# Attention, retention and mixture-of-experts block on one Trainium2 core: the weight slots are cut differently, the record tile gets four buffers, and sixteen identity matmuls stand at the start

## Chip, cores and metric

The kernel is one program on one core of one Trainium2 chip. Its time is device microseconds (us) of one execution. Engines: PE (TensorE; PEld is its weight load), DVE (VectorE), ACT (ScalarE), POOL (GpSimd) and SP (SyncE, which issues nearly all DMAs here, in order, from one queue).

## What is computed

One encoder layer on 512 tokens of width 1024, in float32:

```
xn = rms_norm(x)
proj = xn @ w_in            # attention q/k/v in 3 groups, retention q/k/v/gate, branch gates
A = dilated window attention, 3 groups (window, dilation), 8 heads of 64;
    the groups' outputs are summed with softmax weights of their log-sum-exp
B = retention in chunks of 128, forward + backward, 8 heads, group norm, swish gate
h = x + (sigmoid(gA) * (A @ W_A) + sigmoid(gB) * (B @ W_B)) @ w_out
hn = rms_norm(h)
h = h + MoE(hn)             # 64 experts, top group of 8, top 2 in it; w1, w3: 1024x512, w2: 512x1024
out = rms_norm(h)
```

Every expert's w1, w3 and w2 are read whole: 16 groups of four experts, 12 blocks of 2 MB each.

## The kernel before, in words

**Start.** SP loads the four token tiles `h[:, tt, :]` (128 tokens each, L111) and between them the first two `raw` tiles (512 KB of w_in each, L105). For each token tile ACT squares and sums it (`xs_start`, L223), POOL takes a power (L154), DVE finishes the reciprocal root (L137 to L144) and scales the tile (L232), PE transposes it against `ident` (L196), ACT casts the transposed half (`xH`, L199) and DVE takes the remainder (`xL`, L200). This order is written by hand for DVE, ACT and POOL (`manual_schedule`, L219); everything outside such a block is placed by a list scheduler, which may put other work between. So it is with the retention decays: `dec` is loaded by two small DMAs (L338, L339), and a chain of some 25 small DVE operations (L341 to L357) makes `lg` of it, from which ACT makes the table `xi` (L375). L420 multiplies the router weights `wr` by `nwm`.

**Projections.** `project` multiplies the tokens by 512 columns of a weight matrix. A unit is one `raw` tile (256 rows): ACT makes `wH` (L212), DVE the remainder `wL` (L213), each for two halves of 128 rows (called k0 and k1 here), and PE then runs 24 matmuls: for four accumulators two halves times `x,wH`, `x,wH`, `x,wL` (L267 to L269, or L273 to L275). `raw` has two buffers, `wH` and `wL` three, the accumulators `acc` four. `evac_gate` (L676, ACT) empties the accumulators of a branch gate. The unit spoken of below is the first of branch gate 2, `raw_4115`, `wH_4117`, `wL_4118` in the program before.

**Records.** Attention groups 1 and 2 leave a record (`rec`, 264 KB) per token tile, which goes to DRAM (L660). Between branch gates 1 and 2 the records are combined: per token tile two `rec` are loaded (L697), DVE multiplies three records by their weights (L701), POOL adds the second and the third to the first (L704, two adds), DVE takes a reciprocal (L706) and multiplies (L707). `rec` has two buffers before.

**Experts.** `wtile` hands out slots of 2 MB: first `wA` five times, then `big` and `wk` (each once), then `x0`, `x1` (the tiles that held the transposed tokens) and `wB` twice; after that the ring of nine goes round without `big` and `wk`. A group takes eight blocks of w1 and w3 (j = 0 to 7, L979), then four of w2 (L1049). `wA`, `big` and `wk` lie on the right side of SBUF, in room that the attention's pools leave (`right.close()`, L762); `wk` lay beyond the others, at the edge to the free strip. `x0` and `x1` come free as w_out's matmuls end, `wB` when `mixer.close()` (L918) has given back the left side. Slots are filled in the order in which they are handed out.

Of the kernel before, what the change touches and what calls it, by code (L numbers as in the profile page):

```python
# [10 lines left out]
F32 = mybir.dt.float32  # L11
# [10 lines left out]
P = 128  # L22
# [13 lines left out]
CAP = 32  # L36
EG = 4
NGRP = NE // EG
NWA = 5
NWB = 2  # L40
SLOT = 4096


# [27 lines left out]
def hybrid_block(ctx, tc, a, out):  # L71
# [27 lines left out]
    nc.scalar.dma_start(out=nwx, in_=a["norm_mix_w"].rearrange("o (k p) -> p (o k)", p=P))  # L99
    xp = ctx.enter_context(tc.tile_pool(name="xp", bufs=1, side="left"))  # L100
    lw = mixer.enter_context(tc.tile_pool(name="lw", bufs=1, side="left"))

    def load_raw(w, r0, c0):
        raw = lw.tile([P, 2, 512], F32, name="raw", bufs=2)
        nc.sync.dma_start(out=raw, in_=w[r0:r0 + 2 * P, c0:c0 + 512].rearrange("(k p) n -> p k n", p=P))  # L105
        return raw

# [7 lines left out]
    nc.vector.memset(one1, 1.0)  # L115
    nc.scalar.activation(one1, one1, AF.Square)
    make_identity(nc, ident)
    nc.gpsimd.iota(ranks, pattern=[[1, CAP]], base=1, channel_multiplier=0, allow_small_or_imprecise_dtypes=True)
    nc.gpsimd.iota(iota, pattern=[[1, NE]], base=0, channel_multiplier=0, allow_small_or_imprecise_dtypes=True)
    tri = left.tile([P, P], BF16, name="tri")  # L120
# [501 lines left out]
    for g in range(3):  # L622
        qT, kT = qk_tiles()
        project_in(512 * g, None, rotary_to(qT, g > 0))
        project_in(1536 + 512 * g, None, rotary_to(kT, g > 0, kP))
        vt = rp.tile([P, 2080], F32, name="v", bufs=3)
        v4 = vt.rearrange("p (t h d) -> p t h d", t=NT, h=NH)
        nc.gpsimd.memset(v4[:, :, :, HD:HD + 1], 1.0)

        def evac_va(tt, ps, v4=v4):  # L630
            nc.scalar.copy(v4[:, tt, :, 0:HD], ps.rearrange("p (h d) -> p h d", h=NH))
        project_in(3072 + 512 * g, orders[g], evac_va)

        if g == 0:
            windows(qT, v4)
            continue
        for t in range(NT):
            rec_t = at.tile([P, REC], F32, name="rec", bufs=2)
            rec = rec_t[:, :]
            for h0 in range(0, NH, 4):  # L640
                ps = tmp()
                sm = rp.tile([P, 512], F32, name="sd", bufs=6)
                ts = slice(t * P, (t + 1) * P)
                for i in range(0, 4, 2):
                    nc.tensor.matmul(ps[:, i * P:(i + 2) * P], qT[:, (h0 + i) // 2, ts], kP[:, (h0 + i) // 2, :, ts],  # L645
                                     start=True, stop=True)
                for i in range(4):
                    cs = slice(i * P, (i + 1) * P)
                    probs(rec, h0 + i, ps[:, cs], sm[:, cs],
                          masks[:, 3 * HD:3 * HD + P] if g == 1 else masks[:, 9 * HD:])  # L650
                prT = transposed_probs(ps, sm, 4)
                po_ps = tmp()
                for i in range(4):
                    oc = i * (HD + 1)
                    for f in range(2):
                        qs = slice(i * P + f * HD, i * P + (f + 1) * HD)
                        nc.tensor.matmul(po_ps[f * HD:(f + 1) * HD, oc:oc + HD + 1], prT[:, qs], v4[:, t, h0 + i, :],
                                         start=True, stop=True)
                nc.scalar.copy(rec[:, h0 * (HD + 1):(h0 + 4) * (HD + 1)], po_ps[:, :4 * (HD + 1)])
            nc.sync.dma_start(out=scr[g - 1].rearrange("(l r) c -> r l c", r=4)[t], in_=rec)  # L660
# [32 lines left out]
    for tt in range(NT):  # L693
        r3 = [rec0[:, tt, :]]
        for g in (1, 2):
            rb = at.tile([P, REC], F32, name="rec", bufs=2)
            nc.sync.dma_start(out=rb, in_=scr[g - 1][tt * P:(tt + 1) * P, :])  # L697
            r3.append(rb[:, :])
        r3 = [r_[:, :NH * (HD + 1)].rearrange("p (h d) -> p h d", h=NH) for r_ in r3]
        for g in range(3):  # L700
            nc.vector.tensor_tensor(r3[g], r3[g], al[:, g, tt, :].unsqueeze(2).to_broadcast([P, NH, HD + 1]),  # L701
                                    op=ALU.mult)
        for g in (1, 2):
            nc.gpsimd.tensor_tensor(r3[0], r3[0], r3[g], op=ALU.add)  # L704
        ds = at.tile([P, NH], F32, name="dsum")
        nc.vector.reciprocal(ds, r3[0][:, :, HD])  # L706
        nc.vector.tensor_tensor(yatt[:, tt, :].rearrange("p (h d) -> p h d", h=NH), r3[0][:, :, 0:HD],  # L707
                                ds.unsqueeze(2).to_broadcast([P, NH, HD]), op=ALU.mult)
# [60 lines left out]
    mh = pre.tile([P, NT, NE], BF16, name="mh")  # L769
    big = ctx.enter_context(tc.tile_pool(name="big", bufs=1, side="right"))  # L770
    wA = ctx.enter_context(tc.tile_pool(name="wA", bufs=NWA, side="right"))
    early = ExitStack()
    wk = early.enter_context(tc.tile_pool(name="wk", bufs=1, side="right"))

    def gather(t, oh_t, gp, js=range(NK)):

# [116 lines left out]
    for c in range(2):  # L893
        def evac_o(tt, ps, c=c):
# [10 lines left out]
            else:  # L905
# [4 lines left out]
                    router_rank(tt - 1)  # L910
        project(a["w_out"], 0, NK, 512 * c, mH, mL, nat, evac_o, groups=None if c == 0 else ((0,), (2,), (4, 6)),
                early=True)
    gather_first(1)
    gather_first(2, range(4))
    router_rank(NT - 1)
# [278 lines left out]
```

## Time and profile before

| | |
|---|---|
| runs | 1619.35, 1622.75, 1623.1 us; median 1622.75 |
| profiled execution | 1621.28 us, of which 1619.6 us are the span of the trace |
| PE busy | 1338.7 us (83%) |
| data moved | 476.14 MB, 294 GB/s over the span; 427 to 429 GB/s in nearly every slice from 729 us on |
| chain that ended last | PE 55%, DMA 38%, DVE 4% |

The span falls into two parts. Up to about 680 us PE is busy nearly all the time and the DMA engines are half idle; from about 690 us on the DMA engines are busy all the time and PE partly waits. In the profile's tables a busy share is in tenths of a slice of 40.5 us.

### The profile page before, as it was taken

The numbers are of one execution on the slowest core, as the hardware profiler recorded it, in microseconds if no ns is written. First come the engines' busy times: TensorE is split into PE (matmuls) and PEld (weight loads), VectorE is DVE, ScalarE is ACT, GpSimd is POOL, SyncE is SP. The second block draws the span as 40 slices with busy tenths as digits, with TensorE's granted clock in tenths as the row PEclk, the third lists the DMA queues.
The fourth block names the chain that finished last, engine by engine and source line by source line (L and its number), as shares of the span: only waits on it lengthen the run. The fifth ranks groups of instructions, "written<-read, shape, count | busy, mean of one in ns | idle before, by whom it ended". The sixth has DMA issues, their size and how long they took to land.

```text
span 1619.6 us, 20935 instructions
## 1 busy us (share of the span) xinstructions
PE 1338.7 (83%) x8707; PEld 825.7 (51%) x8707; DVE 562.0 (35%) x1241; ACT 317.8 (20%) x614; POOL 208.4 (13%) x151
## 2 busy tenths in 40 slices
PE   7999999999999999997775785776776676677674
PEld 6878887697977788743331331331332232233133
DVE  7556564464857335441220220221121021022014
ACT  5332333335354423210000000000000000000002
POOL 2213452260716011000000000000000000000001
PEclk9999999999999999999897987998897888898897
DMA  6334243233434423899999999999999999999995
GB/s 183 104 88 108 92 140 96 53 117 93 118 112 133 149 79 132 349 405 428 428 427 429 428 428 428 428 427 429 428 428 428 429 427 429 428 427 428 428 427 224
DMA packets 70980, 476.14 MB, mean 294 GB/s; under 512 B 14240, under 2 KB 14752, under 8 KB 46112
## 3 DMA queue, kind: packets, MB, share of 16 engines
q1 hardware_dynamic: 69840, 474.74, 73.3%
q8 instruction: 70, 1.15, 0.3%
q14 instruction: 30, 0.25, 0.0%
q10 hardware_dynamic: 1040, 0.00, 0.0%
HBM read 459.96 MB, written 4.26 MB: 287 GB/s over the span
## 4 chain that ended last, share of the span: by engine, by line
PE 55%; DMA 38%; DVE 4%; ACT 1%; issue 1%; POOL 1%; SPq 0%; DVEq 0%; ACTq 0%; POOLq 0%
DMA wa<-in_moe_w2r_dram 23%; DMA x<-in_moe_w2r_dram 10%; PE acc L267 6%; PE acc L268 6%; PE acc L269 6%; PE tmp L778 6%; PE acc L979 5%; PE acc L274 4%; PE acc L273 4%; PE acc L275 4%; DMA wa<-in_moe_w_dram 2%; DMA wB<-in_moe_w2c_dram 2%; PE tmp L1031 2%; PE acc L1049 2%; PE tmp L1032 2%; PE tmp L645 1%
## 5 line engine op out<-in xcount | busy, mean ns | idle before, releaser
L979 PE MATMUL acc<-wa,xT 128*32 128x512 f32 x1120 | 156.6, 693 | 69.5 <-DMA wa<-in_moe_w_dram 69.5
L213 DVE SCALAR_TENSOR_TENSOR wL<-raw,nwx,wH 128x512 fp32r<-128x512 f32 x152 | 149.1, 1014 | 118.8 <-ACT wH L212 117.4
L267 PE MATMUL acc<-x,wH 128*128 128x512 f32 x416 | 170.1, 409 | 3.1 <-ACT kT L676 3.1
L269 PE MATMUL acc<-x,wL 128*128 128x512 f32 x416 | 167.8, 403 | 0.0
L268 PE MATMUL acc<-x,wH 128*128 128x512 f32 x416 | 167.8, 403 | 0.0
L212 ACT ACTIVATE wH<-raw,nwx 128x512 fp32r<-128x512 f32 x152 | 103.2, 717 | 174.8 <-PE acc L268 81.3
L1049 PE MATMUL acc<-wa,hid 128*32 128x512 f32 x560 | 88.8, 764 | 54.4 <-DMA wa<-in_moe_w2r_dram 50.2
L274 PE MATMUL acc<-wL,x 128*128 128x512 f32 x320 | 127.8, 399 | 0.1
L273 PE MATMUL acc<-wH,x 128*128 128x512 f32 x320 | 127.4, 399 | 0.1
L275 PE MATMUL acc<-wH,x 128*128 128x512 f32 x320 | 127.4, 398 | 0.0
L154 POOL TENSOR_TENSOR rr<-rv,mhalf 128x1 f32<-128x1 f32 x8 | 5.0, 644 | 925.0 <-ACT jk L1088 914.0
L979 PEld LDWEIGHTS acc<-wa,xT 128*32 128x32 f32 x1120 | 34.2, 119 | 171.4 <-DMA wa<-in_moe_w_dram 93.7
L1011 DVE SCALAR_TENSOR_TENSOR hid<-hid,gsl,acc 128x512 f32<-128x512 f32 x16 | 12.0, 748 | 308.0 <-issue 149.5
L778 PE MATMUL tmp<-oh,h 128*128 128x128 f32 x960 | 111.2, 277 | 0.3 <-DVE big L1033 0.3
L778 PEld LDWEIGHTS tmp<-oh,h 128*128 128x128 f32 x960 | 108.3, 192 | 4.7 <-DVE big L1033 4.7
L1024 DVE TENSOR_TENSOR yp<-acc,yp 128x512 fp32r<-128x512 f32 (+2 forms) x35 | 22.5, 643 | 239.3 <-ACT yp L1023 239.2
L267 PEld LDWEIGHTS acc<-x,wH 128*128 128x128 f32 x416 | 79.1, 190 | 23.5 <-ACT kT L676 3.5
L268 PEld LDWEIGHTS acc<-x,wH 128*128 128x128 f32 x416 | 78.8, 189 | 18.9 <-issue 1.4
L269 PEld LDWEIGHTS acc<-x,wL 128*128 128x128 f32 x416 | 78.8, 189 | 18.0 <-issue 0.2
L979 PE MATMUL acc<-wB,xT 128*32 128x512 f32 x480 | 64.0, 662 | 28.7 <-DMA wB<-in_moe_w_dram 28.7
L979 PE MATMUL acc<-x,xT 128*32 128x512 f32 x416 | 58.8, 702 | 30.0 <-DMA x<-in_moe_w_dram 30.0
L1033 DVE TENSOR_TENSOR big<-big,tmp 128x512 f32<-128x512 f32 (+2 forms) x132 | 76.7, 634 | 14.9 <-PE tmp L1032 14.4
(265 smaller groups left out, 1677.9 us busy)
## 6 DMA issues: line engine op xcount, KB each, us to landing
wa<-in_moe_w_dram SPq DMA_DIRECT2D x70, 2048.0 KB, 39.0
wa<-in_moe_w2r_dram SPq DMA_DIRECT2D x35, 2048.0 KB, 36.2
wB<-in_moe_w_dram SPq DMA_DIRECT2D x30, 2048.0 KB, 39.0
x<-in_moe_w_dram SPq DMA_DIRECT2D x26, 2048.0 KB, 39.1
raw<-in_w_in_dram SPq DMA_DIRECT2D x76, 512.0 KB, 3.5
x<-in_moe_w2r_dram SPq DMA_DIRECT2D x15, 2048.0 KB, 38.9
wB<-in_moe_w2r_dram SPq DMA_DIRECT2D x10, 2048.0 KB, 34.0
sw<-kT SPq DMA_DIRECT2D x32, 128.0 KB, 2.8
```

Of the source, the lines that this page charges most:

```text
L212: nc.scalar.activation(wH[:, k, :], raw[:, k, :], AF.Copy, scale=sc)
L213: nc.vector.scalar_tensor_tensor(wL[:, k, :], raw[:, k, :], sc, wH[:, k, :], op0=ALU.mult, op1=ALU.subtract)
L267: nc.tensor.matmul(ps[tt], wh[:, cs], srcH.blk(kt), **fl)
L268: nc.tensor.matmul(ps[tt], wh[:, cs], srcL.blk(kt), start=False, stop=False)
L269: nc.tensor.matmul(ps[tt], wl[:, cs], srcH.blk(kt), start=False, stop=(kt == nk - 1))
L273: nc.tensor.matmul(ps[tt], aH, wh, **fl)
L274: nc.tensor.matmul(ps[tt], aH, wl, start=False, stop=False)
L275: nc.tensor.matmul(ps[tt], aL, wh, start=False, stop=(kt == nk - 1))
L778: nc.tensor.matmul(gp[j // 4][:, (j % 4) * P:(j % 4 + 1) * P], h[:, t, j * P:(j + 1) * P], oh_t.rearrange("p e c -> p (e c)"), start=(t == ...
L979: nc.tensor.matmul(p_[e * CAP:(e + 1) * CAP, :], xT[:, j, e * CAP:(e + 1) * CAP], wt[:, w_, e, :], start=(j == 0), stop=(j == NK - 1))
L1033: nc.vector.tensor_tensor(hs_[:, t, cs], (h if first else hs_)[:, t, cs], ps, op=ALU.add)
L1049: nc.tensor.matmul(py[hf][e * CAP:(e + 1) * CAP, :], hdT[:, i, e * CAP:(e + 1) * CAP], wt[:, e, hf * 512:(hf + 1) * 512], start=(i == 0), ...
```

## The change

`raw` moves from the pool `lw` to a pool of its own, `lr`, on top of the left side, which is closed (`unsplit.close()`) when w_out's projection has been written down. `wk` is opened only then and so lies in the place of `raw` and of the strip beside it; `wA` gets a sixth buffer, `wB` goes from two to one. The number of slots is eleven as before, in the order six `wA`, `big`, `wk`, `x0`, `x1`, `wB`. `rec` has four buffers. Sixteen matmuls of `ident` with itself follow `make_identity`. Lines of the changed kernel have other numbers: L341 becomes L347, L701 L707, L213 L219, L942 L949.

```diff
-NWA = 5
-NWB = 2
+NWA = 6
+NWB = 1
...
     lw = mixer.enter_context(tc.tile_pool(name="lw", bufs=1, side="left"))
+    unsplit = ExitStack()
+    lr = unsplit.enter_context(tc.tile_pool(name="lr", bufs=1, side="left"))
...
-        raw = lw.tile([P, 2, 512], F32, name="raw", bufs=2)
+        raw = lr.tile([P, 2, 512], F32, name="raw", bufs=2)
...
     make_identity(nc, ident)
+
+    ps = tmp()
+    for _ in range(16):
+        nc.tensor.matmul(ps[:, :P], ident, ident, start=True, stop=True)
...
-            rec_t = at.tile([P, REC], F32, name="rec", bufs=2)
+            rec_t = at.tile([P, REC], F32, name="rec", bufs=4)
...
-            rb = at.tile([P, REC], F32, name="rec", bufs=2)
+            rb = at.tile([P, REC], F32, name="rec", bufs=4)
...
     wA = ctx.enter_context(tc.tile_pool(name="wA", bufs=NWA, side="right"))
-    early = ExitStack()
-    wk = early.enter_context(tc.tile_pool(name="wk", bufs=1, side="right"))
...
         project(a["w_out"], 0, NK, 512 * c, mH, mL, nat, evac_o, groups=None if c == 0 else ((0,), (2,), (4, 6)),
                 early=True)
+    unsplit.close()
+    early = ExitStack()
+    wk = early.enter_context(tc.tile_pool(name="wk", bufs=1, side="right"))
```

The scheduler places work anew. Three places differ; elsewhere in the first 690 us the order of the engines is as before but for details.

DVE at the start, from the second token tile's sum on. Before:

```order
L213 SCALAR_TENSOR_TENSOR wL<-raw,nwx,wH 128x512 x2
L152 TENSOR_SCALAR rv<-ss 128x1
L200 TENSOR_TENSOR x_109<-tmp,x_109 128x4x128
L200 TENSOR_TENSOR x_110<-tmp,x_110 128x4x128
L137 SCALAR_TENSOR_TENSOR rq<-rv,rr 128x1
L142 TENSOR_SCALAR rq<-rq 128x1
L144 TENSOR_TENSOR rr<-rr,rq 128x1
```

DVE at the same place in the changed kernel:

```order
L219 SCALAR_TENSOR_TENSOR wL<-raw,nwx,wH 128x512 x2
L158 TENSOR_SCALAR rv<-ss 128x1
L347 SCALAR_TENSOR_TENSOR dz<-dec 128x16
L362 TENSOR_SCALAR lg<-dec 128x16
L206 TENSOR_TENSOR x_129<-tmp,x_129 128x4x128
L206 TENSOR_TENSOR x_130<-tmp,x_130 128x4x128
L143 SCALAR_TENSOR_TENSOR rq<-rv,rr 128x1
```

The two operations that read `dec` have moved ahead of the first token tile's remainders (before, they stood behind the second tile's). In the same way one `wL` (L219, third `raw`) now stands ahead of the third tile's scaling, and `wr<-wr,nwm` (L426) ahead of the fourth tile's reciprocal root.

DVE where the records are combined, from the second tile's third record on (numbers are those of the tiles; `wL_4118` is the first unit of branch gate 2). Before:

```order
L707 TENSOR_TENSOR qT_4050<-rec0_1608,dsum_4071 128x512
L213 SCALAR_TENSOR_TENSOR wL_4118<-raw_4115,nwx_77,wH_4117 128x512
L701 TENSOR_TENSOR rec_4074<-rec_4074,al_4051 128x520
L701 TENSOR_TENSOR rec_4076<-rec_4076,al_4051 128x520
L213 SCALAR_TENSOR_TENSOR wL_4118<-raw_4115,nwx_77,wH_4117 128x512
```

The same in the changed kernel, where that unit is `wL_4138`:

```order
L707 TENSOR_TENSOR rec_4106<-rec_4106,al_4071 128x520
L713 TENSOR_TENSOR qT_4070<-rec0_1628,dsum_4103 128x512
L707 TENSOR_TENSOR rec_4108<-rec_4108,al_4071 128x520
L707 TENSOR_TENSOR rec0_1628<-rec0_1628,al_4071 128x520
L707 TENSOR_TENSOR rec_4118<-rec_4118,al_4071 128x520
L712 RECIPROCAL dsum_4115<-rec0_1628 128x8
L707 TENSOR_TENSOR rec_4120<-rec_4120,al_4071 128x520
L713 TENSOR_TENSOR qT_4070<-rec0_1628,dsum_4115 128x512
L219 SCALAR_TENSOR_TENSOR wL_4138<-raw_4135,nwx_77,wH_4137 128x512
L712 RECIPROCAL dsum_4127<-rec0_1628 128x8
L219 SCALAR_TENSOR_TENSOR wL_4138<-raw_4135,nwx_77,wH_4137 128x512
```

The unit's `wL` stood behind the first tile's division; now all twelve multiplications and three of the four divisions stand ahead of its k0, and the fourth tile's reciprocal ahead of its k1.

SP from w_out's weights to the first slot that is filled a second time. Before (`x_5660` is x0, `x_5716` x1; `wk` was filled long ago, among the loads of w_in):

```order
L942 DMA wa<-in_moe_w_dram 128x4096
L105 DMA raw<-in_w_out_dram 128x2x512 x2
L942 DMA wa<-in_moe_w_dram 128x4096 x3
L942 DMA big<-in_moe_w_dram 128x4096
L942 DMA x_5660<-in_moe_w_dram 128x4096
L942 DMA x_5716<-in_moe_w2r_dram 128x4096
L942 DMA wB<-in_moe_w2r_dram 128x4096 x2
L942 DMA wa<-in_moe_w2r_dram 128x4096
```

In the changed kernel:

```order
L949 DMA wa<-in_moe_w_dram 128x4096
L107 DMA raw<-in_w_out_dram 128x2x512 x2
L949 DMA wa<-in_moe_w_dram 128x4096 x4
L949 DMA big<-in_moe_w_dram 128x4096
L949 DMA wk<-in_moe_w_dram 128x4096
L949 DMA x_5737<-in_moe_w2r_dram 128x4096
L949 DMA x_5747<-in_moe_w2r_dram 128x4096
L949 DMA wB<-in_moe_w2r_dram 128x4096
L949 DMA wa<-in_moe_w2r_dram 128x4096
```

One more `wa` and `wk` are filled here ahead of x0, and one `wB` is gone. At the records' loads, SP now issues four `rec` at once, then two `raw`, then the other four `rec`; before, two pairs of `raw` stood between the pairs of `rec`.

## Rows read from the trace of the kernel before

**Rows 1.** The page's table of 40 slices: PE's busy tenths, and what the DMA engines moved.
```profile
PE   7999999999999999997775785776776676677674
GB/s 183 104 88 108 92 140 96 53 117 93 118 112 133 149 79 132 349 405 428 428 427 429 428 428 428 428 427 429 428 428 428 429 427 429 428 427 428 428 427 224
```

**Rows 2.** DMA issues of the two decays: queue, count, KB each, us from issue to landing.
```profile
dec<-in_ret_decay_fwd_dram SPq DMA_DIRECT2D x1, 4.0 KB, 7.1
dec<-in_ret_decay_bwd_dram SPq DMA_DIRECT2D x1, 4.0 KB, 6.2
```

**Rows 3.** The timeline of SP at the start: start, duration, operation.
```profile
6.15 0.43 SPq L338 DMA_DIRECT2D dec<-in_ret_decay_fwd_dram  x1
7.23 0.33 SPq L339 DMA_DIRECT2D dec<-in_ret_decay_bwd_dram  x1
```

**Rows 4.** The timeline of DVE at the start (in brackets, where there is any, idle time before and what ended it).
```profile
10.55 1.27 DVE L200 TENSOR_TENSOR x<-tmp,x 128x512 fp32r<-128x512 f32 x2
...
15.88 0.17 DVE L341 SCALAR_TENSOR_TENSOR dz<-dec 128x16 f32<-128x16 f32 x1
...
17.44 0.66 DVE L213 SCALAR_TENSOR_TENSOR wL<-raw,nwx,wH 128x512 fp32r<-128x512 f32 x1
...
20.60 0.88 DVE L232 TENSOR_SCALAR v<-h,rr 128x512 f32<-128x512 f32 x2
...
24.27 0.75 DVE L420 TENSOR_TENSOR wr<-wr,nwm 128x576 f32<-128x576 f32 x1
```

**Rows 5.** The timeline of PE at the start: the transposes of the four token tiles' first (8.23) and last (21.74), and matmuls between.
```profile
8.23 2.19 PE L196 MATMUL tmp<-ident,v 128*128 128x128 f32 x8 [8.23 <-DVE v L232]
...
10.80 0.63 PE L274 MATMUL acc<-wL,x 128*128 128x512 f32 x1
11.29 0.79 PE L275 MATMUL acc<-wH,x 128*128 128x512 f32 x1
...
13.04 0.39 PE L273 MATMUL acc<-wH,x 128*128 128x512 f32 x1
...
21.74 1.03 PE L196 MATMUL tmp<-ident,v 128*128 128x128 f32 x8
```

**Rows 6.** The timeline of DVE at the records.
```profile
499.61 1.92 DVE L701 TENSOR_TENSOR rec<-rec,al 128x520 f32<-128x520 f32 x3 [0.35 <-ACT al L692]
501.44 1.81 DVE L701 TENSOR_TENSOR rec<-rec,al 128x520 f32<-128x520 f32 x1
503.18 1.80 DVE L701 TENSOR_TENSOR rec<-rec,al 128x520 f32<-128x520 f32 x1
...
505.58 0.68 DVE L707 TENSOR_TENSOR qT<-rec,dsum 128x512 f32<-128x512 f32 x1
...
508.07 1.80 DVE L213 SCALAR_TENSOR_TENSOR wL<-raw,nwx,wH 128x512 fp32r<-128x512 f32 x1
```

**Rows 7.** The timeline of POOL at the records.
```profile
501.05 3.37 POOL L704 TENSOR_TENSOR rec<-rec,rec 128x520 f32<-128x520 f32 x2 [2.27 <-DVE rec L701]
...
522.07 1.32 POOL L704 TENSOR_TENSOR rec<-rec,rec 128x520 f32<-128x520 f32 x1 [0.69 <-DVE rec L701]
```

**Rows 8.** The timeline of PE at the first unit of branch gate 2 (511.37 is its third matmul, the first that reads `wL`; 521.08 is the next unit's first).
```profile
511.37 0.40 PE L269 MATMUL acc<-x,wL 128*128 128x512 f32 x1
...
514.87 0.39 PE L269 MATMUL acc<-x,wL 128*128 128x512 f32 x1
518.36 0.79 PE L267 MATMUL acc<-x,wH 128*128 128x512 f32 x1 [3.10 <-ACT kT L676]
...
521.08 0.57 PE L267 MATMUL acc<-x,wH 128*128 128x512 f32 x1
521.50 0.39 PE L268 MATMUL acc<-x,wH 128*128 128x512 f32 x1
```

**Rows 9.** The timelines of SP and of ACT at the same place.
```profile
502.72 8.66 SPq L697 DMA_DIRECT2D rec<-scr  x4
511.49 2.25 SPq L105 DMA_DIRECT2D raw<-in_w_in_dram  x2
517.01 0.72 ACT L212 ACTIVATE wH<-raw,nwx 128x512 fp32r<-128x512 f32 x1 [6.62 <-DMA raw<-in_w_in_dram]
517.64 0.67 ACT L676 ACTIVATE kT<-acc,bg 128x512 f32<-128x512 f32 x1
```

**Rows 10.** Busy time by stretch: stretch, us, then PE, PEld, DVE, ACT and POOL busy (instructions), the granted clock, the DMA engines' share, GB/s.
```profile
518.00:520.00 2.00, 1.64 (x4) 1.35 (x5) 2.00 (x4) 0.92 (x2) 0.30 (x1) 0.51 0.55 149
...
680.00:690.00 10.00, 9.49 (x78) 6.98 (x77) 8.60 (x46) 2.97 (x7) 1.11 (x2) 1.00 0.26 79
690.00:700.00 10.00, 9.43 (x97) 7.78 (x99) 8.40 (x49) 1.53 (x10) 0.55 (x1) 1.00 0.93 387
```

**Rows 11.** The timeline of SP where the slots are first filled, and of DVE at the last `raw`'s split.
```profile
524.49 0.33 SPq L942 DMA_DIRECT2D wk<-in_moe_w_dram  x1
668.10 1.23 DVE L208 TENSOR_TENSOR wL<-raw,wH 128x1024 fp32r<-128x1024 f32 x1 [4.96 <-ACT wH L207]
672.50 0.33 SPq L942 DMA_DIRECT2D x<-in_moe_w_dram  x1
688.72 0.33 SPq L942 DMA_DIRECT2D x<-in_moe_w2r_dram  x1
700.32 0.33 SPq L942 DMA_DIRECT2D wa<-in_moe_w2r_dram  x1
```

## The prediction, made before the changed kernel ran

> **What bounds the kernel now.** I read the page's 40 slices first. PE is busy in nine tenths of nearly every slice up to the seventeenth, and the DMA engines move about a third of what they can; from the eighteenth on they stand at 427 to 429 GB/s in every slice and PE is at six or seven tenths [rows 1]. So until about 690 us PE sets the time, then the DMA engines do, and the turn is where the change works on the weight slots. Both parts count in full: a us lost by PE ahead of the turn delays every expert load that waits for room, since the slots behind x0 come free only as PE finishes w_out; a us in which the DMA engines stand still after the turn is lost too. Next I read the places where the order differs: the start (SP, DVE, PE) [rows 2 to 5], the records (DVE, POOL, PE, SP, ACT) [rows 6 to 9], and the turn [rows 10, 11]. The profiled execution took 1621.28 us; the median of the runs is 1622.75, 1.5 above it.
>
> **The start: +3.9 us.** The two decay tiles are issued at 6.15 and 7.23 [rows 3] and land 7.1 and 6.2 us after issue [rows 2]: at 13.25 and 13.43. Before, their first reader on DVE runs at 15.88, when they have long landed; the remainders of the first token tile run at 10.55 [rows 4]. In the changed order two readers of `dec` stand ahead of these remainders. DVE works in order, so it gets to them at 10.55, waits until 13.43, spends 0.17 on each (the length of the L341 row; the second is of the same shape) and begins the remainders at about 13.7: 3.15 late. Behind the waiting operation stand all of DVE's start, and PE: the matmul at 11.29 multiplies `xL` [rows 5], which these remainders make. PE then idles some 3.1 us. Two more operations move ahead of work that PE waits for: one wL, 0.66, ahead of the third tile's scaling, and `wr<-wr,nwm`, 0.75, ahead of the fourth tile's root [rows 4]. Against this, the last transposes begin at 21.74 [rows 5], while their tile is scaled by 21.48 (20.60 and the second of two at 0.88 [rows 4]): 0.25 of slack, which is used up first. And PE has two matmuls fewer behind the last transposes (58, not 60), 0.46 at the 0.233 us that a matmul takes below. Sum 3.15 + 0.66 + 0.75 − 0.25 − 0.46 = 3.85. Ends: 2.4 with the late `dec` alone and both credits, 4.6 with the three terms and no credit.
>
> The sixteen identity matmuls cost nothing: at the 0.27 of one of eight cold transposes (2.19 us for them) they take 4.4 us, and PE's first work waits 8.23 us for DVE [rows 5]. Can they gain? In the trace the first eight transposes take 2.19 us and the last eight 1.03, and the matmuls at 10.80 and 11.29 take 0.63 and 0.79, against 0.39 at 13.04 [rows 5]: PE begins at a low clock. But what it then waits for is DVE, so I take 0. The Trainium skill (TensorE: Matmul & The Clock Gate, Part 1: The HAM clock gate) says that the throttled clock is the default and that activity releases it. By that rule the identity matmuls would free the clock before the first transposes, and the start would cost 1.3 us instead of 3.9 where PE is the pace (2.6 less, worked out under the rivals). The trace agrees on the slow start; no run so far shows what early matmuls do to it.
>
> **The records: +4.5 us.** Four `rec` buffers let SP issue four loads at once. Before, SP was held for 8.66 us in its four `rec` loads, so the next `raw` was issued only at 511.49; ACT waited 6.62 us for it, with the evacuation of the last branch gate (kT, 517.64) behind that wait [rows 9]; PE idled 3.10 us on that evacuation [rows 8]. With four buffers `raw` goes early and this stall ends. Taken alone this gives 3.10 plus the slow clock behind it: the granted clock is 0.51 at 518 to 520 [rows 10], the 1.2 GHz level.
>
> What comes late next is `wL`. PE needs the unit's k0 for its third matmul, at 511.37 [rows 8]. Before, k0 and k1 came early in DVE's order (k1 at 508.07 [rows 6]); now k0 stands behind all twelve multiplications and three divisions, k1 behind the fourth reciprocal, which waits for POOL's eighth add. How fast does DVE get through? Multiplications next to POOL's adds take 1.80 and follow each other at 1.74 (501.44 to 503.18); alone such an operation takes 0.68 [rows 6]. POOL's add takes 1.32 alone and 1.68 in a pair [rows 7]. The two engines hold each other. In the changed order seven DVE operations from 501.44 on run beside an add (12.2 us at 1.74) and five alone (3.4 at 0.68), so k0 begins at 517.0 and, held by an add itself, ends at 518.8; k1 follows within a us. PE has then idled from 511.37 to about 518.7. 22 matmuls of the unit are left. The wait of 3.10 us was followed by seven starts in 3.14 us (518.36 to 521.50), so I take seven at that pace; the other fifteen go at the pace of 511.37 to 514.87, fifteen in 3.50 [rows 8]. Next unit at 518.7 + 6.6 = 525.3, and 525.9 with k1 last: +4.2 to +4.8 against 521.08. Upper end 5, with both. Lower end: were DVE not held by POOL, k0 would stand at about 510.5 and k1 at 512.5; PE would wait under a us and the next unit begin at 517.4: −3.7. I take the upper half, since [rows 6] and [rows 7] show the holding on this very code. The next `raw` needs the buffer that this late unit frees, is issued at about 520 and needed at 531; before, a wait like that of 6.62 came only when the issue was late by as much. No further stall.
>
> **The turn: −3.0 us.** At 680 to 690 the DMA engines moved 79 GB/s and at 690 to 700 387, of 428 [rows 10]: 349/428 × 10 + 41/428 × 10 = 9.1 us lost. SP had issued x0 at 672.50 and had to wait to 688.72 for x1 [rows 11]. A slot of 2 MB takes 4.90 us at 428 GB/s. Now six `wA`, `big` and `wk` come before x0, with one load more of `wA` and that of `wk`, 9.8 us, in this hole; `wk` has to wait for the last split of `raw`, which ends at 669.3 (668.10 + 1.23 [rows 11]), some 10 us before the queue would run dry. So the engines are busy until 691.4; x1, free at 688.7, follows without a gap, then one `wB` to 701.2. The first second use of a `wA` was issued at 700.32 [rows 11] and takes up to 2 us to begin: 1.2 lost. But the load of `wk` was free before, at 524.49 among the weights of w_in [rows 11], while the DMA engines had room; now its 4.9 us lie in the part that DMA bounds. −9.1 + 4.9 + 1.2 = −3.0. Ends: −4.2 if the reuse comes in time, 0 if the hole only moves to behind `wB`. In the steady state nine slots go round as before, at a full 428.
>
> **Sum.** 3.9 + 4.5 − 3.0 = +5.4: 1626.7 against the profiled execution, 1628.2 against the median. I forecast **1627**, between the two and nearer to the one whose rows were summed. A measurement of this kernel can tell about 0.3%, 4.9 us, from no change, so the forecast itself lies near that bound.
>
> **Rivals.**
> - **DVE and POOL do not hold each other** as I count, or the scheduler's place for `wL` costs nothing: the records give −3.7. For it: the reciprocals are short and POOL's adds have gaps (2.27 [rows 7]). Against: 1.80 for operations beside adds [rows 6]. 3.9 − 3.7 − 3.0 = −2.8: 1619.
> - **`dec` is not late:** it decides from a landing under about 3.3 us after issue, where the trace has 7.1 and 6.2 [rows 2]. Or DVE's first work is itself later. The start then costs 0 to 1. 4.5 − 3.0 + 0.5: 1623 to 1624.
> - **The early clock counts:** PE sets the pace of the start, and the first transposes take 1.03 instead of 2.19 and some seven matmuls 0.2 less each [rows 5], 2.6 in all. For it: the difference is in the rows. Against: PE waits for DVE there. 5.4 − 2.6 = +2.8: 1624. This is the Trainium skill's rule from above.
> - **Both new orders go unfelt**: no wait on `dec`, none on `wL`, the hole filled: −3.7 − 3.0 and up to 1 from the clock: 1615, faster..
> - **The hole moves instead of closing** (slower): with one `wB` the queue has no slot between x1 and the second use of the first `wA`. Before, that use was issued 11.6 us after x1 (688.72 to 700.32 [rows 11]). If it comes 14.6 us after x1, because the experts' first matmuls now meet slots in another order, the 1.2 us become 4.2 and the gain is gone. +8.4: 1630.
>
> **How the numbers follow.** Forecast as summed 0.55, with a range of its own of 1624 to 1630, of which 62% lies beyond the bound on the slow side; no hold between DVE and POOL 0.15; `dec` not late 0.08; early clock 0.04; both orders unfelt 0.08; the hole moves 0.10. Slower by over 0.3%: 0.34 + 0.10 = 0.44. Faster: 0.08. Within: 0.48. The range of 1619 to 1631 leaves out the fastest case and half of the one at 1619.
>
> **What would show it.** Right at the start: DVE idle that ends on the `dec` load at 13.4, PE idle of some 3 us before the first matmul that reads `xL`, last transposes at about 25.5. Right at the records: no wait of ACT on `raw`, a PE idle of about 7 us that ends on `wL`, the 1.2 GHz level behind it. Right at the turn: no 10 us under 300 GB/s between 680 and 700 (later by the time lost ahead), x1 issued before the engines run dry, a hole of 1 to 2 us before the first reuse. Wrong: PE's unit after the records begins earlier than 521 + 3.8, which makes the holding of DVE by POOL the failed step; or a hole of over 4 us behind `wB`; or a rate after 730 us other than 428 GB/s, which I have not counted at all.

## The result: 8.3 us slower

The changed kernel takes 1631.24 us (median of six runs, 1629.87 to 1632.8), the kernel before 1622.92 (six runs): a ratio of 1.0053 with a 95% interval of 1.0044 to 1.0063, that is 7 to 10 us. The forecast was 1627 with a range up to 1631, so the direction of the sum (+5.4) was right and its size was too small. The profiled execution took 1632.8 us, the longest of the six, so single terms are read from it and their sum is judged by the medians.

The profile after, the page's busy tenths of PE and rates in 40 slices (40.8 us each), against [rows 1]: the DMA-bound part is as dense as before, the first part reads alike.

```profile
PE   8999999999998999998877776886777677777575
GB/s 173 101 94 99 91 142 98 58 103 98 124 99 122 105 78 96 411 416 427 427 429 430 426 428 429 427 427 429 428 428 428 429 428 428 427 429 428 427 428 182
```

**Start.** DVE's timeline, against [rows 4] (start, duration, operation, idle time before it and what ended it):

```profile
13.44 0.18 DVE L347 SCALAR_TENSOR_TENSOR dz<-dec 128x16 f32<-128x16 f32 x1 [2.85 <-DMA dec<-in_ret_decay_bwd_dram]
13.54 0.17 DVE L362 TENSOR_SCALAR lg<-dec 128x16 f32<-128x16 f32 x1
13.61 1.28 DVE L206 TENSOR_TENSOR x<-tmp,x 128x512 fp32r<-128x512 f32 x2
```

PE's timeline, against [rows 5]: the identity matmuls, the first transposes, the wait for `xL`, the transposes of the second and of the fourth token tile.

```profile
1.52 5.95 PE L123 MATMUL tmp<-ident 128*128 128x128 f32 x32 [1.52 <-POOL ident masks.py:199]
8.10 0.66 PE L202 MATMUL tmp<-ident,v 128*128 128x128 f32 x4 [0.63 <-DVE v L238]
...
10.40 0.40 PE L280 MATMUL acc<-wL,x 128*128 128x512 f32 x1
14.35 0.79 PE L281 MATMUL acc<-wH,x 128*128 128x512 f32 x1 [3.56 <-DVE x L206]
14.94 0.63 PE L279 MATMUL acc<-wH,x 128*128 128x512 f32 x1
...
16.65 1.91 PE L202 MATMUL tmp<-ident,v 128*128 128x128 f32 x8
...
26.98 1.06 PE L202 MATMUL tmp<-ident,v 128*128 128x128 f32 x8
```

The reader should see three things. `dec` lands when the prediction had it land (forecast 13.43), and DVE waits 2.85 us for it with `xL` behind. PE is at full speed before that wait (four transposes in 0.66, where eight took 2.19 before; 0.40 a matmul) and at half speed after it (0.63, and 1.91 for eight transposes). The last transposes come at 26.98, 5.24 later than in [rows 5]. Two matmuls that stood behind them now stand ahead of them, so at 30 us PE is 4.83 us late, counted to the same place in its sequence of matmuls.

**Records.** DVE's timeline, against [rows 6], from the first multiplication to the unit's `wL` (the list of DVE's changed order above begins at the third tile's second record, 515.14 here):

```profile
505.59 5.38 DVE L707 TENSOR_TENSOR rec<-rec,al 128x520 f32<-128x520 f32 x5 [0.35 <-ACT al L698]
...
511.57 1.81 DVE L713 TENSOR_TENSOR qT<-rec,dsum 128x512 f32<-128x512 f32 x1
...
515.71 0.68 DVE L713 TENSOR_TENSOR qT<-rec,dsum 128x512 f32<-128x512 f32 x1
...
522.70 1.76 DVE L219 SCALAR_TENSOR_TENSOR wL<-raw,nwx,wH 128x512 fp32r<-128x512 f32 x1
```

PE's timeline, against [rows 8]; 524.51 is the unit's third matmul, 531.42 the next unit's first:

```profile
516.54 0.40 PE L274 MATMUL acc<-x,wH 128*128 128x512 f32 x1
524.51 0.79 PE L275 MATMUL acc<-x,wL 128*128 128x512 f32 x1 [7.58 <-DVE wL L219]
525.10 0.63 PE L273 MATMUL acc<-x,wH 128*128 128x512 f32 x1
...
531.42 0.39 PE L273 MATMUL acc<-x,wH 128*128 128x512 f32 x1
```

In this unit ACT no longer waits for `raw`; `wL` is what is late. (ACT's next wait for a `raw`, 11.62 us up to 528.82, belongs to a later unit, and PE does not stop for it.) The next unit begins 10.34 us after 521.08. PE had come to this unit 5.40 late (516.54 + 0.23 against 511.37), so the records cost 4.94.

**Turn.** SP's timeline against [rows 11] (the second `x` of the pair, x1, goes at the end of the 16.56 us), and the stretches against [rows 10] (columns as there):

```profile
651.10 0.34 SPq L949 DMA_DIRECT2D wa<-in_moe_w_dram  x1
...
679.69 0.33 SPq L949 DMA_DIRECT2D wk<-in_moe_w_dram  x1
682.84 16.56 SPq L949 DMA_DIRECT2D x<-in_moe_w2r_dram  x2
...
710.66 0.33 SPq L949 DMA_DIRECT2D wa<-in_moe_w2r_dram  x1
```

```profile
690.00:700.00 10.00, 9.46 (x76) 6.92 (x75) 8.55 (x46) 2.62 (x7) 1.11 (x2) 1.00 1.02 432
700.00:710.00 10.00, 9.43 (x96) 8.01 (x99) 8.40 (x48) 1.53 (x7) 0.55 (x1) 1.00 0.99 416
710.00:720.00 10.00, 10.00 (x100) 3.12 (x96) 4.26 (x33) 2.81 (x11) 0.00 (x0) 1.00 0.97 387
```

The hole of 79 GB/s is gone; (428 − 416)/428 × 10 + (428 − 387)/428 × 10 = 1.2 us remain, as forecast. PE's delay of 10.34 is there undiminished in the first late `wa` issue (651.10 against 640.76 in the kernel before). That issue is the marker for the whole first part below; the first store of the result (1607.03 before, 1618.55 after) is the marker for the end. Both markers before, then the store after:

```profile
640.76 0.34 SPq L942 DMA_DIRECT2D wa<-in_moe_w_dram  x1
...
1607.03 6.78 SPq L1128 DMA_DIRECT2D out_dram<-wa  x6
```
```profile
1618.55 6.78 SPq L1135 DMA_DIRECT2D out_dram<-wa  x6
```

### The profile page after: what moved, and what is told of

It reads as the page before. It is cut to its first block, busy times and chain, and to the rows that moved or that the text cites. A ratio compares the mean times of both kernels' runs of the same rounds, so it can differ in the third digit from the quotient of the medians.

```text
span 1631.1 us, 20990 instructions
## 1 busy us (share of the span) xinstructions
PE 1368.8 (84%) x8739; PEld 838.5 (51%) x8739; DVE 568.9 (35%) x1241; ACT 318.0 (19%) x614; POOL 208.6 (13%) x151
## 4 chain that ended last, share of the span: by engine, by line
PE 53%; DMA 39%; DVE 4%; issue 1%; POOL 1%; ACT 1%; SPq 0%; DVEq 0%; ACTq 0%; POOLq 0%
DMA wa<-in_moe_w2r_dram 18%; DMA x<-in_moe_w2r_dram 12%; PE acc L273 6%; PE acc L275 6%; PE acc L274 6%; PE tmp L782 5%; PE acc L986 5%; PE acc L281 4%; PE acc L280 4%; PE acc L279 4%; DMA x<-in_moe_w_dram 2%; DMA wB<-in_moe_w_dram 2%; DMA wa<-in_moe_w_dram 2%; PE acc L1056 2%; PE tmp L1038 2%; PE tmp L1039 2%
## 5 line engine op out<-in xcount | busy, mean ns | idle before, releaser
L986 PE MATMUL acc<-wa,xT 128*32 128x512 f32 x1376 | 194.9, 703 | 79.7 <-DMA wa<-in_moe_w_dram 79.6
L219 DVE SCALAR_TENSOR_TENSOR wL<-raw,nwx,wH 128x512 fp32r<-128x512 f32 x152 | 150.0, 1020 | 123.9 <-ACT wH L218 122.4
L1056 PE MATMUL acc<-wa,hid 128*32 128x512 f32 x640 | 104.6, 784 | 66.8 <-DMA wa<-in_moe_w2r_dram 64.3
L986 PEld LDWEIGHTS acc<-wa,xT 128*32 128x32 f32 x1376 | 42.7, 120 | 211.3 <-issue 105.0
L1056 PEld LDWEIGHTS acc<-wa,hid 128*32 128x32 f32 x640 | 21.1, 125 | 142.2 <-issue 70.3
L274 PEld LDWEIGHTS acc<-x,wH 128*128 128x128 f32 x416 | 78.8, 189 | 18.9 <-issue 1.4
L322 POOL TENSOR_TENSOR sw<-sw,ropeT 128x512 f32<-128x512 f32 x28 | 51.9, 1876 | 206.1 <-DMA sw<-qT 113.2
```

Of the source, the lines that this page charges most:

```text
L219: nc.vector.scalar_tensor_tensor(wL[:, k, :], raw[:, k, :], sc, wH[:, k, :], op0=ALU.mult, op1=ALU.subtract)
L274: nc.tensor.matmul(ps[tt], wh[:, cs], srcL.blk(kt), start=False, stop=False)
L986: nc.tensor.matmul(p_[e * CAP:(e + 1) * CAP, :], xT[:, j, e * CAP:(e + 1) * CAP], wt[:, w_, e, :], start=(j == 0), stop=(j == NK - 1))
L1056: nc.tensor.matmul(py[hf][e * CAP:(e + 1) * CAP, :], hdT[:, i, e * CAP:(e + 1) * CAP], wt[:, e, hf * 512:(hf + 1) * 512], start=(i == 0), ...
```

## Experiments

"Part one" is the shift of the first late `wa` issue against 640.76, "rest" the further shift up to the first store, both from one profiled execution. Times are medians, each against runs of the kernel before on the same chip; different rows are in part from different chips.

| run | us | ratio [95%] | part one | rest |
|---|---|---|---|---|
| changed kernel | 1631.24 | 1.0053 [1.0044, 1.0063] | +10.34 | +1.18 |
| slots_only | 1622.03 | 0.9992 [0.9982, 1.0002] | +0.62 | −0.38 |
| ident_only | 1624.23 | 1.0005 [0.9996, 1.0015] | +1.83 | −0.12 |
| rec4_only | 1627.09 | 1.0027 [1.0018, 1.0036] | +7.02 | +0.86 |
| no_ident | 1625.98 | 1.0025 [1.0013, 1.0036] | +5.88 | −1.20 |
| ident_decay_later | 1622.22 | 0.9996 [0.9987, 1.0005] | +0.92 | +0.38 |
| ident_decay_third | 1621.59 | 0.9990 [0.9981, 0.9999] | −0.01 | −0.02 |
| rec4_wl_first | 1621.02 | 0.9991 [0.9983, 1.0000] | −1.86 | −0.08 |
| rec4_adds_on_dve | 1619.38 | 0.9980 [0.9971, 0.9990] | −1.14 | +0.66 |
| adds_on_dve_only | 1618.67 | 0.9972 [0.9962, 0.9982] | −4.37 | +0.76 |
| slots_wl_first | 1617.11 | 0.9972 [0.9962, 0.9982] | −1.10 | −1.09 |
| slots_rec4_adds | 1617.39 | 0.9969 [0.9956, 0.9982] | −3.35 | −1.02 |
| after_adds_decay | 1616.82 | 0.9962 [0.9949, 0.9974] | −2.86 | −1.13 |

The theory after the result: the loss is the two waits of the start and of the records, each with a slow clock behind it, less a gain at the turn. Rivals: the parts lose only together; the identity matmuls themselves, the four buffers or the ring with one `wB` lose.

### Each part alone

The slots alone:

```diff
-NWA = 5
-NWB = 2
+NWA = 6
+NWB = 1
...
-        raw = lw.tile([P, 2, 512], F32, name="raw", bufs=2)
+        raw = lr.tile([P, 2, 512], F32, name="raw", bufs=2)
...
+    unsplit.close()
+    early = ExitStack()
+    wk = early.enter_context(tc.tile_pool(name="wk", bufs=1, side="right"))
```

> The slot part alone (raw in a pool of its own, wk in its place, six wA, one wB); record buffers and start as before. Theory: the changed kernel's three parts add up, and this one gives back what the other two lose: the stretch of 680 to 692 us in which the DMA engines stood still closes (9 us), wk's load costs 4.9, 1.3 remain open, so 2 to 3 us less than before, about 1620.3, with no 10 us under 380 GB/s between 670 and 720. Rival: what the turn gains is lost again behind it, in the ring with one wB or at the end of the last group, and the time is that of before, 1622.9, or above.

Measured −1.0 us, inside the interval of no change. The hole closes (424 and 428 GB/s at 680 to 700, 375 behind it), and the bulk of the DMA engines' stream ends some 2 us earlier; but the last block that PE waits for arrives no earlier, as the tail of the two kernels shows below. The theory's size was too large; the rival's "nothing" isn't excluded by this run alone.

The identity matmuls alone:

```diff
     make_identity(nc, ident)
+    ps = tmp()
+    for _ in range(16):
+        nc.tensor.matmul(ps[:, :P], ident, ident, start=True, stop=True)
```

> The sixteen identity matmuls alone. Theory: the scheduler places the two readers of dec ahead of the first tile's remainders because of them, DVE waits for dec to 13.4 us, PE idles 3.5 us and restarts at 1.2 GHz: 5 to 5.4 us more than before, about 1628, all of it lost by 30 us. Rival: the late dec belongs to the combination with the other parts, and alone the matmuls cost nothing or gain 1 to 3 us: 1620 to 1623.

Measured +1.2 (ratio: +0.8). The theory missed: the order of DVE and the wait are there (PE idle 3.46 at 14.41, ended by `xL`), but part one ends up only 1.83 late. PE reaches the records 4.12 late and leaves the first unit 1.47 late: the stall there is shorter. PE's and ACT's timelines and the clock there:

```profile
521.24 0.50 PE L271 MATMUL acc<-x,wH 128*128 128x512 f32 x1 [1.85 <-ACT kT L680]
```
```profile
519.89 0.72 ACT L216 ACTIVATE wH<-raw,nwx 128x512 fp32r<-128x512 f32 x1 [5.37 <-DMA raw<-in_w_in_dram]
```
```profile
520.00:522.00 2.00, 0.76 (x3) 0.68 (x4) 0.35 (x2) 1.80 (x3) 1.50 (x2) 1.00 0.78 229
```

PE's wait is 1.85 instead of 3.10 [rows 8], because the late `raw`, issued 4.52 later than in [rows 9] (516.01), reached ACT only 2.88 later; and after 1.85 the granted clock is still 1.00, where it was 0.51 after 3.10 [rows 10]. It is not PE's delay that shortens the stall: with the identity matmuls and the readers of `dec` where they were (ident_decay_third below) PE comes to it only 0.82 late, and the stall is 1.93. The three kernels with identity matmuls and two record buffers all have this shorter stall; what makes their `raw` land sooner isn't known.

Four record buffers alone:

```diff
-            rec_t = at.tile([P, REC], F32, name="rec", bufs=2)
+            rec_t = at.tile([P, REC], F32, name="rec", bufs=4)
...
-            rb = at.tile([P, REC], F32, name="rec", bufs=2)
+            rb = at.tile([P, REC], F32, name="rec", bufs=4)
```

> Four record buffers alone. Theory: wL of the first unit of branch gate 2 stands behind twelve multiplications, PE waits some 7.6 us on it instead of 3.1 on the evacuation: 5 us more, about 1628. Rival: DVE reaches that wL late only because the start was late or the slots differ; alone the early raw wins and the time is 3 us below before, about 1620.

Measured +4.1 (1.0027: 3 to 6 us), with the wait on `wL` at the same place (6.70 us): the theory holds, the rival falls.

### Do the parts add?

The changed kernel without the identity matmuls:

```diff
-    ps = tmp()
-    for _ in range(16):
-        nc.tensor.matmul(ps[:, :P], ident, ident, start=True, stop=True)
```

> The changed kernel without the sixteen identity matmuls (slots and four record buffers stay). Theory: the identity matmuls cost little alone (1.2 us in their own run) only because the stall that follows at the records took up what the start lost; with four record buffers that stall is of another kind and does not shrink, so in the changed kernel they cost the full 4 to 5 us: 1626 to 1627. Rival: they cost 1 us here too, and two thirds of the loss is due to something that only the three parts together do, 1630.

Measured 1625.98: the identity matmuls cost 5 us in the changed kernel and 1 alone. PE waits 7.08 us for `wL` here and 7.58 in the changed kernel: this wait follows PE's own delay, since DVE's chain begins with it, and takes nothing up. The theory's time holds. Its reason for the small cost alone, a stall that takes up what the start lost, does not: the stall is shorter without the loss too.

### The start

The identity matmuls, with DVE's two readers of `dec` behind the last token tile's remainder, then behind the second's. The edit for the second (the first has no `if`):

```diff
-            transpose_split(xs[:, :D], xH, xL, slice(tt * P, (tt + 1) * P), NK)
+            xl = transpose_split(xs[:, :D], xH, xL, slice(tt * P, (tt + 1) * P), NK)
+            if tt == 1:
+                last_xl = xl
...
-        nc.vector.scalar_tensor_tensor(z, dec, -1.0, dec, op0=ALU.mult, op1=ALU.min)
+        with tc.issue_after(last_xl.ins):
+            nc.vector.scalar_tensor_tensor(z, dec, -1.0, dec, op0=ALU.mult, op1=ALU.min)
```

(The other reader, `lg<-dec`, likewise; `transpose_split` returns its last operation.)

> The identity matmuls, with the two readers of dec issued behind the last token tile's remainder on DVE. Theory: the loss of the identity matmuls was the wait on dec and the slow clock behind it, so both go: PE has no idle over 1 us between 10 and 20 us, and its first transposes and matmuls run at 2.4 GHz, 1 to 2.6 us less than before: 1620.3 to 1622. Rival: DVE paces the start whatever PE's clock is, and the time is that of before, 1622.9. Rival two: the identity matmuls themselves are in the way, and 3 us or more stay lost, 1626 or above.

> The identity matmuls alone, with the two readers of dec issued behind the second token tile's remainders, where the kernel before has them. Theory: without the wait on dec PE has no idle over 1 us after 9 us and runs at 2.4 GHz from its first transposes, yet DVE paces the start, so at 45 us PE stands within 1 us of before and the time is 1622 to 1623.5. Rival: PE's clock paces the start, and 2 to 3 us are gained: 1620.

Measured 1622.22 and 1621.59. The 3.5 us of PE's idle are gone in both. In the second PE is warm from its first transposes on, and still waits for DVE:

```profile
8.32 0.66 PE L200 MATMUL tmp<-ident,v 128*128 128x128 f32 x4
9.49 0.66 PE L200 MATMUL tmp<-ident,v 128*128 128x128 f32 x4 [0.52 <-DVE v L237]
...
11.47 0.51 PE L282 MATMUL acc<-wH,x 128*128 128x512 f32 x1 [0.83 <-DVE x L204]
```

At 45 us PE stands 0.54 us behind the kernel before, and part one is where it was (−0.01). The identity matmuls raise the clock and gain no time at the start, since DVE paces it: the theory holds. In the first of the two runs DVE works at the decay chain, pushed behind the tokens, from 26.4 to 34.2, the rotary operations come late (PE waits 0.98, 0.40 and 0.84 us on them, at 39.66 to 45.45), and PE is 2.7 us late at 45 us; only the shorter stall at the records (1.85) brings part one back to 0.9.

### The records

Wait for POOL or wait for the order? First, wL ahead of the records of tiles 1 to 3, with four buffers:

```diff
+    n0 = len(wls)
+    branch_gate(2, "v")
     for tt in range(NT):
...
         for g in range(3):
-            nc.vector.tensor_tensor(r3[g], r3[g], al[:, g, tt, :].unsqueeze(2).to_broadcast([P, NH, HD + 1]),
-                                    op=ALU.mult)
+            with tc.issue_after(wls[n0 + 2 * tt - 1].ins) if tt else ExitStack():
+                nc.vector.tensor_tensor(r3[g], r3[g], al[:, g, tt, :].unsqueeze(2).to_broadcast([P, NH, HD + 1]),
+                                        op=ALU.mult)
...
-    branch_gate(2, "v")
```

(`wls` collects the `wL` operations as they are written down.)

> Four record buffers alone, and on DVE the multiplications of record tiles 1, 2 and 3 are issued behind the first, second and third unit's wL of branch gate 2 (which is written down ahead of the records). Theory: the loss of the four buffers was the place of wL in DVE's order; with wL early neither the late raw nor the late wL stops PE, it idles under 1 us near 515 us and stays at 2.4 GHz: 3 to 4.5 us less than before, 1618.5 to 1620. Rival: another wait takes over at the same place (SP behind the record loads, POOL's adds, the evacuation), 1623 or above.

Measured 1621.02, ratio 0.9991 [0.9983, 1.0000]. At the first unit neither wait is left; PE then waits 1.80 us at 536.13 on an evacuation (L678) that stands in ACT's order behind a `wH` which itself waited 9.31 us for PE to free its buffer. The rival is half right: another wait takes over, smaller and later.

Second, POOL's adds on DVE:

```diff
-            nc.gpsimd.tensor_tensor(r3[0], r3[0], r3[g], op=ALU.add)
+            nc.vector.tensor_tensor(r3[0], r3[0], r3[g], op=ALU.add)
```

> Four record buffers alone, and POOL's eight adds of the records are done by DVE. Theory: DVE's operations take 1.75 us there only while POOL adds; without POOL each takes 0.65 to 0.7, so DVE does eight operations more and still ends the first unit's wL no later: the stretch from the first multiplication to that wL's end, 18.9 us with POOL's adds, is 16 to 17 us, and PE's idle falls from 6.7 to 4 to 5 us. Rival: the operations are slow by themselves (the broadcast operand, 520 columns): they stay at 1.7, the stretch grows to 25 us or more and PE's idle beyond 11 us.

> The kernel before with POOL's eight adds of the records on DVE, two record buffers as before. Theory: the root of the stall at the records is that POOL's adds and DVE's operations hold each other (the record buffers come free late, SP stands behind them); with DVE alone the records are done in 15 us, raw is issued some 3 us earlier and PE's idle of 3.10 falls under 1: 1619 to 1620.5, as with four buffers and the adds on DVE. Rival: two buffers are what holds SP whoever adds, the idle stays at 2 to 3 us and the time at 1622 to 1623.

Measured 1619.38 with four buffers, 1618.67 with two. DVE's timeline with four buffers, first multiplication, a division, the unit's `wL`:

```profile
502.51 1.92 DVE L701 TENSOR_TENSOR rec<-rec,al 128x520 f32<-128x520 f32 x3 [0.35 <-ACT al L692]
504.35 0.69 DVE L704 TENSOR_TENSOR rec<-rec,rec 128x520 f32<-128x520 f32 x1
...
507.47 0.68 DVE L707 TENSOR_TENSOR qT<-rec,dsum 128x512 f32<-128x512 f32 x1
...
516.13 0.74 DVE L213 SCALAR_TENSOR_TENSOR wL<-raw,nwx,wH 128x512 fp32r<-128x512 f32 x1
```

Multiplications, adds and divisions take 0.65 to 0.69 and `wL` 0.74, none 1.8. DVE does eight operations more, seven of them ahead of this `wL`, and from the first multiplication to the end of `wL` it needs 14.4 us (502.51 to 516.87) instead of 18.9 (505.59 to 524.46 in the changed kernel, the same in rec4_only). PE's idle falls to 0.70. This settles that POOL's adds held DVE's operations; the theory was too careful with 16 to 17 us and an idle of 4 to 5. The Trainium skill (GPSIMD Engine Reference, 1. Specifications) says that GpSimd's SBUF interfaces are shared with VectorE and contend with DVE instructions that have two SBUF inputs. These runs agree: 1.8 beside an add, 0.69 without.

With two buffers the timelines of SP and of ACT read:

```profile
502.43 5.93 SPq L697 DMA_DIRECT2D rec<-scr  x3
508.70 0.38 SPq L105 DMA_DIRECT2D raw<-in_w_in_dram  x1
```
```profile
512.60 1.34 ACT L212 ACTIVATE wH<-raw,nwx 128x512 fp32r<-128x512 f32 x2 [0.41 <-DMA raw<-in_w_in_dram]
```

`raw` goes 2.79 us earlier than in [rows 9], ACT waits 0.41 for it instead of 6.62, PE doesn't idle there. Two buffers are enough once POOL is out of the way.

### Together

Three sums of the edits above: slots, four buffers and `wL` first; slots, four buffers and the adds on DVE; and the changed kernel whole, with the adds on DVE and the readers of `dec` behind the second tile's remainders (cut; the other lines as above):

```diff
-            nc.gpsimd.tensor_tensor(r3[0], r3[0], r3[g], op=ALU.add)
+            nc.vector.tensor_tensor(r3[0], r3[0], r3[g], op=ALU.add)
...
+        with tc.issue_after(last_xl.ins):
```

> The slot part and four record buffers with wL first, no identity matmuls. Theory: the gains add, 3 to 4.5 at the records and 1 to 2 at the turn: 1617 to 1619. Rival: the slots' gain at the turn is swallowed at the end of the last group, where the last block lands no earlier, and the time is that of the run with wL first alone.

> The changed kernel without identity matmuls and with the adds of the records on DVE. Theory: 3.3 us at the records as in the run with four buffers and DVE's adds, and 1 to 2 at the turn: 1617 to 1618.5. Rival: the slots give nothing once the records are mended: 1619.4.

> The changed kernel whole, with the adds of the records on DVE and the two readers of dec behind the second tile's remainders: both waits that it brought are taken away. Theory: the 8.3 us were these two waits less the turn's gain, so nothing of the loss is left and the time is that of the same kernel without identity matmuls, within 1 us: 1616.5 to 1618.5. Rival: a part of the loss has another root (the tail of the last group, the ring with one wB), and the time stays at 1621 or above.

Measured 1617.11, 1617.39 and 1616.82, the last with a ratio of 0.9962 [0.9949, 0.9974], the fastest kernel run. All three times lie in the theory's ranges. In the first the parts did not add as the theory had it: wL first had gained 1.6 alone, not 3 to 4.5, and with the slots its wait of 1.80 us at 536.13 is missing. The last run shows that the two waits are the loss: with them taken away the same slots, buffers and identity matmuls are 6 us faster than before. The adds on DVE gained 4.4 alone and the slots 1 to 2, which leaves no room for a hidden loss of more than about a us.

## Why the prediction fell short

- **What bounds**: right. What part one loses arrives at the end in the changed kernel. (The rate is full from the nineteenth slice of [rows 1], not the eighteenth, which has 405; nothing hangs on it.)
- **Start, +3.9 forecast, 4.8 measured at 30 us** (at the last transposes, ahead of the credit for two matmuls, 4.3 and 5.2). Wait and place were right: `xL` begins at 13.61 (forecast 13.7), PE idles 3.56 (3.1). What failed is the step from the idle to the sum. Behind the 3.10 us idle at the records the prediction charged a slow clock; behind the idle of the same length at the start it charged none, because it took DVE to be the pace. PE ran at 1.2 GHz from 14.35 to 19.6, and DVE then waited for the second tile's transposes (1.91 for 1.03) through ACT's casts. The granted clock by stretches after:

```profile
10.00:12.00 2.00, 0.74 (x2) 0.30 (x2) 0.60 (x2) 2.00 (x5) 0.56 (x1) 1.00 1.07 369
...
14.00:16.00 2.00, 1.65 (x4) 1.36 (x5) 1.90 (x7) 0.00 (x0) 0.00 (x0) 0.50 1.03 365
```

What this cost is read on DVE's timeline, the second tile's remainders before, then the same and the early `wL` after:

```profile
14.56 1.28 DVE L200 TENSOR_TENSOR x<-tmp,x 128x512 fp32r<-128x512 f32 x2
```
```profile
18.36 0.69 DVE L206 TENSOR_TENSOR x<-tmp,x 128x512 fp32r<-128x512 f32 x1 [0.65 <-ACT x L205]
19.21 0.69 DVE L206 TENSOR_TENSOR x<-tmp,x 128x512 fp32r<-128x512 f32 x1 [0.16 <-ACT x L205]
...
20.88 0.75 DVE L219 SCALAR_TENSOR_TENSOR wL<-raw,nwx,wH 128x512 fp32r<-128x512 f32 x1 [0.46 <-ACT wH L218]
```

The first tile's remainders begin 3.06 us late (10.55 to 13.61), the second tile's end 4.06 late (15.84 to 19.90): the slow clock cost 1.00, which the prediction put at nothing. The early `wL` cost 1.10 by the third tile's scaling (16.42 to 21.55), 0.46 of it a wait for ACT that was not counted, and `wr` 0.61; the slack gave back 0.50 and the two matmuls 0.41. The rest of the 5.4 that PE is late at the records is not the start's: kernels with the start as before lose 0.4 to 0.5 there too (adds_on_dve_only, no_ident).

- **Identity matmuls at nothing**: right, in cost and in gain, once `dec` is not late: they take 5.95 us (estimated 4.4) and end before PE's first work, and the changed kernel with both waits mended takes 1616.82 with them and 1617.39 without. The Trainium skill's rule that was weighed (TensorE: Matmul & The Clock Gate, Part 1: The HAM clock gate) agrees on the clock: the first transposes run at full speed. It didn't become time.
- **Records, +4.5 forecast, 4.94 measured**: right; nine slow matmuls follow the wait, not seven.
- **Turn, −3.0 forecast**: the hole closed as forecast (9.1 to 1.2), and the stream of loads gained as forecast. Counted over the packets of the traces, all but the last 8 MB of what is moved ahead of the first store has landed 2.7 to 3.1 us earlier, part one deducted, in all six kernels with the slots, and within 0.3 us of before in the seven others. What failed is the step from there to the end: −1.0 to −1.2 arrives as "rest" in four of the six, −0.4 in slots_only. One stretch of the tail, the kernel before and then the slots alone:

```profile
1590.00:1592.00 2.00, 1.87 (x64) 1.60 (x64) 0.40 (x2) 1.21 (x7) 0.00 (x0) 1.00 0.90 365
```
```profile
1590.00:1592.00 2.00, 2.00 (x66) 1.69 (x65) 0.95 (x3) 1.69 (x8) 0.00 (x0) 1.00 0.54 217
```

The rate falls to half some 2 us earlier with the slots (before, it is at 246 GB/s in the next stretch), yet the block whose load PE waits for last comes at the same time in both, on PE's timeline, the kernel before and then the slots alone:

```profile
1594.79 1.95 PE L1040 MATMUL acc<-wB,hid 128*32 128x128 f32 x64 [0.87 <-DMA wB<-in_moe_w2c_dram]
```
```profile
1595.03 1.95 PE L1043 MATMUL acc<-wB,hid 128*32 128x128 f32 x64 [0.85 <-DMA wB<-in_moe_w2c_dram]
```

The traces record 16 landings for each load, as many as there are DMA engines, and these lie far apart at the end. Of this `wB` the first landing is at 1586.69 before and 1584.46 with the slots alone, the last at 1594.75 and 1594.99. With part one deducted the first comes 2.9 to 3.4 us earlier in the six kernels with the slots, the last only 0.4 to 1.8; from first to last it is 9.6 to 10.5 us there and 8.0 to 8.4 without the slots, against 2 to 3 us where a slot is first filled a second time, near 700 us. PE needs the last. In eight of the thirteen kernels the "rest" is the shift of this last landing to 0.01 us; in the other five it is larger. The prediction let the mean rate say when a block is complete. Why the landings drift apart, and further with the hole closed, stays open.

- **The sum**: 4.8 + 4.9 = 9.7, and the 8.3 of the medians leave −1.4 for the turn, within what the traces show of it. In the profiled execution the last landing of `wB` gained 1.78 (part one deducted), but the rest is +1.18: the last group ran at the low clock, and PE, not the load, was late there:

```profile
1580.00:1590.00 10.00, 6.99 (x36) 1.21 (x32) 0.00 (x0) 0.00 (x0) 0.00 (x0) 0.50 1.01 433
1590.00:1600.00 10.00, 8.01 (x82) 4.55 (x75) 1.60 (x3) 1.43 (x3) 0.00 (x0) 0.50 0.94 399
```

The 2.96 between the two, with 5.40, 4.94 and −1.78, make the 11.52 by which this execution is longer than that of [rows 1]. Three others had a shorter stretch at the low clock at that place, and their rest is 0.8 to 0.9 above the shift of the last landing (rec4_only, rec4_adds_on_dve, adds_on_dve_only). By medians, kernels with the slots stand 1.0, 1.1, 2.0 and 3.9 us below the same kernels without them (1622.03, 1625.98, 1617.39 and 1617.11 against the runs of before, rec4_only, rec4_adds_on_dve and rec4_wl_first); the last has the missing wait at 536.13 in it.
- **The rivals**: "DVE and POOL do not hold each other" fell by the runs with the adds on DVE. "`dec` is not late" and "both new orders go unfelt" fell by the trace, "the early clock counts" by the run with the readers of `dec` where they were (PE warm, 0.54 behind at 45 us). "The hole moves" gave the nearest time, 1630, by a mechanism that didn't occur: luck, as the hole closed.

## What to carry to other kernels

A wait is priced with the clock behind it wherever it stands, also where another engine seems to set the pace: here a us. A rate averaged over 16 engines does not say when a block is complete; the last of its landings does. Adding a few instructions anywhere can make a list scheduler move others: sixteen matmuls on an idle engine cost 5 us through two DVE operations of 0.17 us each. Before a buffer is added for a late release, ask what makes the release late: one word (the adds on DVE instead of POOL) gained 4.4 us where two more buffers lost 4.1.

## What the runs showed beyond this

- Costs of parts did not add: 1.2 + 4.1 − 1.0 = 4.3 alone, 8.3 together, because the kernels with identity matmuls have a shorter stall at the records as long as `rec` has two buffers (PE 4.12 late ahead of it, 1.47 behind), and with four buffers there is no such stall.
- Three runs with identity matmuls and two buffers waited 1.85 to 1.93 us at the records, the kernel before and the slots alone 3.10 and 3.04; the two `raw` issued there landed 3.5 to 3.8 us after issue in the former, 4.8 to 5.4 and 4.4 to 5.0 in the latter. Why isn't settled.
- The clock behind a wait of some 1.15 us near 143.5 differs between executions of the same instructions. In rec4_only it fell and PE lost 2.4 us between 143 and 150 (so without it part one would be some 4.6 late, not 7.0); in no_ident it didn't. It fell in slots_wl_first too, in none of the other twelve. The stretch in rec4_only, then in no_ident:

```profile
148.00:152.00 4.00, 4.00 (x19) 4.00 (x20) 0.23 (x2) 0.58 (x1) 2.50 (x2) 0.50 0.01 5
```
```profile
148.00:152.00 4.00, 4.00 (x33) 3.67 (x32) 1.53 (x10) 1.17 (x2) 2.50 (x2) 1.00 0.04 13
```

So a difference of 2 us in part one between single profiled executions of this kernel tells nothing by itself; the place where it arises must be read.
